# Column sums of two RMS norms: a product with a column of ones, or a transpose and a sum on VectorE

## The chip, the cores and the metric

The kernel runs on one core of a Trainium2 chip. The metric is the device time of one execution in microseconds, as the median of several runs. The engines are TensorE (PE in the profile; PEld is its weight load), VectorE (DVE), ScalarE (ACT), GpSimd (POOL) and SyncE (SP), which here only issues DMAs.

## The reference

One layer of a hybrid model is computed for a prompt of 2048 tokens and a step of 64 tokens, in FP32, with a model width of 1024:

```python
h = rms_norm(x, g_pre)
proj = einsum('btd,dn->btn', h, w_in)              # ten blocks of 1024 columns
...                                                # short convolution (yA), gated recurrence (yB)
merged = sigmoid(gA) * yA + sigmoid(gB) * yB
out = einsum('btd,de->bte', merged, w_o)
x = x + rms_norm(out, g_post)
gate = sigmoid(einsum('btd,de->bte', rms_norm(x, g_ple), w_ple_gate))
x = x + einsum('btp,pd->btd', p, w_ple_proj) * gate

def rms_norm(x, g):
    return x * rsqrt(mean(x * x, axis=-1) + 1e-6) * g
```

The change is in the two norms between w_o and w_ple_gate: the one by g_post and the one by g_ple.

## The kernel before

The 2112 tokens stand side by side and are cut into three blocks of 704, each into two segments (halves) of 352. Activations lie with features on the 128 partitions and tokens along the free axis; a width of 1024 is eight tiles of 128 features. FP32 products are made of three matmuls each on a high and a low part (hi by hi, hi by lo, lo by hi), and large products by a scheme of seven half-size products (functions sgroup, from line 348, and in_turn, from line 469; the three matmuls of one product are lines 362 to 364, 495 to 497 and 528 to 530). Weights come from memory, are split into high and low parts, and the low parts and operand sums of the first block are kept in memory for the later ones.

A norm over features is a sum over partitions here. It is made in steps:

- sum_squares squares the eight feature tiles on ScalarE (lines 634 and 637) and adds them up on VectorE (line 638) into acc, a tile of 128 partitions by tokens.
- col_rstd sums acc over its partitions. For 352 tokens there are three tiles of 128 columns (tiles_of; the third overlaps the second). Each tile is the stationary operand of a product with a column of ones, line 619, so that a column of PSUM gets the sums of 128 tokens, one to a partition. The tokens' sums end as 128 partitions by 3 columns in pc.
- rstd_of scales by 1/1024 and adds epsilon on VectorE (line 590), then takes the power -0.5 on GpSimd (line 592).
- spread (line 603) transposes each column, broadcast to 128x128, so that every partition holds the factor of every token; a copy (line 629, on ScalarE, in the last block on VectorE) brings it to SBUF.
- final_norm multiplies by it: line 1185 with g_post, 1186 adds x, then the second norm, 1199 with g_ple.

rms calls col_rstd once for each segment it is given, and yields between the sums and the spread. In the first and the second block both segments are normed together; in the last block each is normed by itself, so that there are 12 calls of col_rstd.

These steps don't run as a stage of their own. They are handed out by spread_out as hooks, called between the matmuls of the products that follow: in the first two blocks during the gate products of the next block (the first of its stages, lines 362 to 364), in the last block during the end of the W_O products (lines 495 to 497) and during the W_G products of the block before (final_gate, lines 528 to 530). The order on each engine is set by a planner that goes through the program with modelled times and takes by priority what is ready; issue_after pins an instruction behind another on the same engine. With it, placed() queues the products of col_rstd and of spread right behind the last matmul traced before them. DMAs are issued by SP (weights) and by GpSimd (activations, spills, results).

PSUM has five banks for the products (tag pg) and three for everything else (tag pa); pc is one of the latter.

Of the kernel before, what the change touches and what calls it, by code (L numbers as in the profile page):

```python
# [10 lines left out]
F32 = mybir.dt.float32  # L11
# [3 lines left out]
ALU = mybir.AluOpType  # L15
# [3 lines left out]
P = 128  # L19
D = 1024  # L20
# [62 lines left out]
def hybrid_step(  # L83
# [17 lines left out]
    V, A, G, T, SP = nc.vector, nc.scalar, nc.gpsimd, nc.tensor, nc.sync  # L101
# [3 lines left out]
    const = ctx.enter_context(tc.tile_pool(name="const", bufs=1))  # L105
# [13 lines left out]
    def rt(n=BN, dt=F32):  # L119
        t = ring.tile([P, BN + 4], dt, tag="r", name=nm("r"))  # L120
        return t if n is None else t[:, :n]
# [4 lines left out]
    def ps_attn():  # L126
        return psa.tile([P, 512], F32, tag="pa", name=nm("pa"))
# [7 lines left out]

    ident = const.tile([P, P], F32, tag="ident", name="ident")
    make_identity(nc, ident)
    ones = const.tile([P, 1], F32, tag="ones", name="ones")
    V.memset(ones, 1.0)
    mhalf = const.tile([P, 1], F32, tag="mhalf", name="mhalf")  # L140
    V.memset(mhalf, -0.5)
    vec = const.tile([P, 9, KB], F32, tag="vec", name="vec")
# [98 lines left out]
    def placed():  # L241

        return tc.issue_after(last[0]) if last[0] is not None else nullcontext()
# [341 lines left out]
    def tiles_of(n):  # L585

        return [(i, min(i * P, n - P)) for i in range((n + P - 1) // P)]

    def rstd_of(ms_ap, out_ap, scale, start=0):
        scaled = V.tensor_scalar(out_ap, ms_ap, scale, EPS, ALU.mult, ALU.add).ins  # L590
        shape = [out_ap.shape[0], out_ap.shape[1]]
        G.tensor_tensor(out_ap, out_ap, mhalf[start : start + shape[0], :].to_broadcast(shape), ALU.pow)
        return scaled

    def cols_tile(n):
        return small.tile([P, (n + P - 1) // P], F32, tag=f"cols{n}", name=nm("cols"))

    def spread(cols, n):

        pb = ps_attn()  # L600
        with placed():
            for i, o in tiles_of(n):
                T.transpose(pb[:, o : o + P], cols[:, i : i + 1].to_broadcast([P, P]), ident)
        return pb[:, :n]
# [8 lines left out]
    def col_rstd(acc, n):  # L613

        pc = ps_attn()
        cols = cols_tile(n)
        with placed():
            for i, o in tiles_of(n):
                T.matmul(pc[:, i : i + 1], acc[:, o : o + P], ones, start=True, stop=True)
        rstd_of(pc[:, : cols.shape[1]], cols, 1.0 / D)  # L620
        return cols

    def rms(acc, out, segs, copy=A.copy):


        cols = [col_rstd(acc[:, cols_of(sg)], sg["n"]) for sg in segs]
        yield
        for sg, col in zip(segs, cols):
            copy(out[:, cols_of(sg)], spread(col, sg["n"]))
        yield  # L630
# [248 lines left out]
    def cols3(t, nt):  # L879
        return t[:, : nt * P].rearrange("p (g c) -> p g c", c=P)  # L880
# [464 lines left out]
    with behind_all(done):  # L1345
        rs = rt()
        cols = [spread(ss[:, 0, 3 * h : 3 * h + 3], HN) for h in range(2)]
# [22 lines left out]
    for bi, bl in enumerate(blocks):  # L1370
# [6 lines left out]
        cols, a_first = [], []  # L1377
# [18 lines left out]
        mg, xo, h2, acc = [], [], [], rt()  # L1396
# [99 lines left out]
```

## Time and profile before

| | |
|---|---|
| median of three runs | 2632.4 us (2630.19 to 2634.68) |
| profiled execution | 2636.6 us, its span 2634.9 us |
| TensorE busy | 2600.3 us |
| VectorE busy | 1666.3 us |
| ScalarE busy | 1538.5 us |
| GpSimd busy | 386.9 us |

Busy times are of the profiled execution. Times in rows of the timeline are microseconds from the span's start. The first norm begins at 870 us, the last ends at 2539 us. A row of a group gives line, engine, operation, output and inputs by the program's names, the count, and the durations in ns; a row of the timeline gives start, length and what ended the engine's idle time before it, in square brackets.

### The profile page before, as it was taken

The numbers are of one execution on the slowest core, as the hardware profiler recorded it, in microseconds if no ns is written. First come the engines' busy times: TensorE is split into PE (matmuls) and PEld (weight loads), VectorE is DVE, ScalarE is ACT, GpSimd is POOL, SyncE is SP. The second block draws the span as 40 slices with busy tenths as digits, with TensorE's granted clock in tenths as the row PEclk, the third lists the DMA queues.
The fourth block names the chain that finished last, engine by engine and source line by source line (L and its number), as shares of the span: only waits on it lengthen the run. The fifth ranks groups of instructions, "written<-read, shape, count | busy, mean of one in ns | idle before, by whom it ended". The sixth has DMA issues, their size and how long they took to land.

```text
span 2634.9 us, 47400 instructions
## 1 busy us (share of the span) xinstructions
PE 2600.3 (99%) x16550; PEld 2582.7 (98%) x16550; DVE 1666.3 (63%) x3233; ACT 1538.5 (58%) x2948; POOL 386.9 (15%) x713
## 2 busy tenths in 40 slices
PE   7999999999999999999999999999999999999999
PEld 7999999999999999999999999999999999999998
DVE  7687887898777555455545568553455544479656
ACT  5666666554334644677745556466667745565636
POOL 1000000200432210011112211021000101210220
PEclk9999999999999999999999999999999999999999
DMA  8678778898988997767789989599777789989967
GB/s 290 220 262 283 246 269 278 298 316 291 332 299 283 350 328 257 244 224 226 223 288 358 386 306 313 187 363 346 230 228 222 223 258 345 379 308 308 329 234 240
DMA packets 364912, 749.14 MB, mean 284 GB/s; under 512 B 44832, under 2 KB 49472, under 8 KB 364672
## 3 DMA queue, kind: packets, MB, share of 16 engines
q1 hardware_dynamic: 322560, 584.00, 65.2%
q0 software_dynamic: 41824, 162.06, 16.8%
q8 instruction: 130, 2.13, 0.3%
q14 instruction: 110, 0.90, 0.1%
q10 hardware_dynamic: 288, 0.05, 0.0%
HBM read 534.88 MB, written 211.04 MB: 283 GB/s over the span
## 4 chain that ended last, share of the span: by engine, by line
PE 92%; DMA 3%; DVE 2%; issue 1%; ACT 1%; POOL 0%; SPq 0%; ACTq 0%; DVEq 0%; POOLq 0%
PE pg L362 19%; PE pg L364 19%; PE pg L363 19%; PE pg L529 5%; PE pg L530 5%; PE pg L528 5%; PE pg L495 4%; PE pg L496 4%; PE pg L497 4%; PE pa L980 1%; PE pa L944 1%; PE pa L982 1%; PE pa L930 1%; DMA raw<-S 1%; DMA r<-x_fm 1%
## 5 line engine op out<-in xcount | busy, mean ns | idle before, releaser
L362 PE MATMUL pg<-r,hi 128*128 128x352 f32 x3304 | 1094.8, 331 | 4.2 <-DVE r L408 2.6
L363 PE MATMUL pg<-r,hi 128*128 128x352 f32 x3304 | 1068.0, 323 | 0.0
L364 PE MATMUL pg<-r,lo 128*128 128x352 f32 x2356 | 763.2, 324 | 2.2 <-DMA lo<-low 2.2
L218 ACT CAST hi<-raw 128x512 fp32r<-128x512 f32 x720 | 444.3, 619 | 498.8 <-PE pg L363 167.3
L362 PEld LDWEIGHTS pg<-r,hi 128*128 128x128 f32 x3304 | 623.0, 189 | 9.0 <-DVE r L408 4.0
L363 PEld LDWEIGHTS pg<-r,hi 128*128 128x128 f32 x3304 | 623.3, 189 | 0.0
L364 PEld LDWEIGHTS pg<-r,lo 128*128 128x128 f32 x2356 | 443.6, 188 | 2.9 <-DMA lo<-low 2.8
L364 PE MATMUL pg<-r,s 128*128 128x352 f32 x948 | 307.2, 324 | 0.0
L529 PE MATMUL pg<-r,hi 128*128 128x352 f32 x768 | 249.5, 325 | 0.0
L528 PE MATMUL pg<-r,hi 128*128 128x352 f32 x768 | 249.3, 325 | 0.1
L188 ACT CAST hi<-raw 128x512 fp32r<-128x512 f32 x218 | 134.3, 620 | 152.9 <-PE pg L363 46.1
L188 DVE TENSOR_TENSOR r<-r,r 128x352 fp32r<-128x352 f32 (+3 forms) x298 | 183.1, 636 | 63.8 <-ACT r L188 62.9
L496 PE MATMUL pg<-r,hi 128*128 128x352 f32 x672 | 217.3, 325 | 0.0
L495 PE MATMUL pg<-r,hi 128*128 128x352 f32 x672 | 213.6, 325 | 0.1
L530 PE MATMUL pg<-r,lo 128*128 128x352 f32 x656 | 213.0, 325 | 0.0
L188 ACT CAST r<-r 128x352 fp32r<-128x352 f32 (+3 forms) x298 | 161.9, 578 | 61.9 <-DVE r L671 17.4
L188 DVE TENSOR_TENSOR lo<-raw,hi 128x512 fp32r<-128x512 f32 x218 | 149.3, 686 | 68.1 <-ACT hi L188 59.3
L364 PEld LDWEIGHTS pg<-r,s 128*128 128x128 f32 x948 | 178.6, 188 | 0.0
L188 ACT CAST hi<-s 128x512 fp32r<-128x512 f32 x160 | 98.1, 619 | 123.8 <-PE pg L363 112.8
L376 ACT COPY hf<-pg 128x352 f32<-128x352 f32 x354 | 157.0, 446 | 12.2 <-PE pg L364 11.6
L529 PEld LDWEIGHTS pg<-r,hi 128*128 128x128 f32 x768 | 145.2, 189 | 0.4 <-DVE r L188 0.3
L528 PEld LDWEIGHTS pg<-r,hi 128*128 128x128 f32 x768 | 145.1, 189 | 0.4 <-ACT r L188 0.4
(372 smaller groups left out, 4160.5 us busy)
## 6 DMA issues: line engine op xcount, KB each, us to landing
raw<-w_blk SPq DMA_DIRECT2D x570, 256.0 KB, 4.2
lo<-low SPq DMA_DIRECT2D x411, 256.0 KB, 4.4
raw<-S SPq DMA_DIRECT2D x408, 256.0 KB, 4.4
low<-lo SPq DMA_DIRECT2D x322, 256.0 KB, 3.7
s<-low SPq DMA_DIRECT2D x309, 256.0 KB, 4.2
S<-s SPq DMA_DIRECT2D x160, 256.0 KB, 3.1
r<-w_blk POOLq DMA_DIRECT2D x64, 256.0 KB, 7.2
S<-r POOLq DMA_DIRECT2D x64, 256.0 KB, 5.9
```

The lines of the kernel that those rows point to most:

```text
L188: return A.copy(hi, src).ins, V.tensor_tensor(lo, src, hi.bitcast(F32), ALU.subtract).ins
L218: A.copy(hi, raw)
L362: add(hi[:, k, :], xhi, start=start and k == 0, stop=False)
L363: add(hi[:, k, :], xlo, start=False, stop=False)
L364: last[0] = add(lo[:, k, :], xhi, start=False, stop=k == KH - 1).ins
L376: copied = A.copy(got[n], ps[bank])
L495: add(hi[:, k, :], xhi, start=start and k == 0, stop=False)
L496: add(hi[:, k, :], xlo, start=False, stop=False)
L497: last[0] = add(lo[:, k, :], xhi, start=False, stop=k == KH - 1).ins
L528: T.matmul(ps, hi[:, k % 4, :], xhi[:, c], start=k == ks[0], stop=False)
L529: T.matmul(ps, hi[:, k % 4, :], xlo[:, c], start=False, stop=False)
L530: last[0] = T.matmul(ps, lo[:, k % 4, :], xhi[:, c], start=False, stop=k == ks[-1]).ins
```

## The change

Each tile of acc is transposed into PSUM (128 columns for each of the three tiles), so that a token's squares lie along the free axis of one partition; VectorE then adds up each 128, writes 128x3 sums to cols in SBUF, and rstd_of works on cols. The column of ones goes.

```diff
-    ones = const.tile([P, 1], F32, tag="ones", name="ones")
-    V.memset(ones, 1.0)
...
         with placed():
             for i, o in tiles_of(n):
-                T.matmul(pc[:, i : i + 1], acc[:, o : o + P], ones, start=True, stop=True)
-        rstd_of(pc[:, : cols.shape[1]], cols, 1.0 / D)
+                T.transpose(pc[:, i * P : i * P + P], acc[:, o : o + P], ident)
+        nt = cols.shape[1]
+        V.tensor_reduce(cols, cols3(pc, nt), axis=mybir.AxisListType.X, op=ALU.add)
+        rstd_of(cols, cols, 1.0 / D)
         return cols
```

cols3 (line 879 of the kernel before) views the first nt x 128 columns of a tile as 128 x nt x 128.

## The prediction

> **What bounds the kernel now.** I read the profile page first, then the group of each line that the change touches, then the stretches of the timeline around them.
>
> ```profile
> span 2634.9 us, 47400 instructions
> PE 2600.3 (99%) x16550; PEld 2582.7 (98%) x16550; DVE 1666.3 (63%) x3233; ACT 1538.5 (58%) x2948; POOL 386.9 (15%) x713
> PE 92%; DMA 3%; DVE 2%; issue 1%; ACT 1%; POOL 0%; SPq 0%; ACTq 0%; DVEq 0%; POOLq 0%
> ```
>
> TensorE is busy for 99% of the span and makes 92% of the chain that ended last; VectorE has 37% of its time free. So a microsecond taken from TensorE's queue is worth a microsecond wherever TensorE does not then wait for something else, and a microsecond given to VectorE is free unless TensorE waits for its result. The change moves work in exactly that direction.
>
> The lines it touches, by their groups (duration columns are ns min/median/max):
>
> ```profile
> L619 PE MATMUL pa<-ones,r x72: 164/250/353, 870.4 to 2533.1; 128*128 128x1 f32 x72
> L603 PE MATMUL pa<-ident,cols x48: 270/272/421, 793.7 to 2538.8; 128*128 128x128 f32 x48
> L987 DVE TENSOR_REDUCE ms<-r x24: 679/686/689, 123.8 to 2115.7; 128x4 f32<-128x512 f32 x24
> L987 DVE TENSOR_REDUCE ms<-one x24: 276/278/284, 129.9 to 2119.9; 128x1 f32<-128x128 f32 x24
> L590 DVE TENSOR_SCALAR cols<-pa x12: 155/160/163, 871.3 to 2533.5; 128x3 f32<-128x3 f32 x12
> ```
>
> The code calls col_rstd for each of two segments in two norms of three blocks: 12 calls of 3 tiles, 36 products by ones. The trace has 72, so each FP32 product is two passes. The same code's spread (L603) asks for 54 transposes in all and shows 48 under cols, the rest (first block) under another name: a transpose is one pass. It is the very instruction that the change adds, in shape and type.
>
> **What goes and comes on TensorE.** Durations overlap, so I take the pitch: the time by which the next ordinary matmul is late. Timeline of the first norm, both segments together:
>
> ```profile
> 870.15 0.32 PE L363 MATMUL pg<-r,hi 128*128 128x352 f32 x1
> 870.44 1.47 PE L619 MATMUL pa<-ones,r 128*128 128x1 f32 x12
> 872.01 0.32 PE L362 MATMUL pg<-r,hi 128*128 128x352 f32 x1
> ...
> 874.26 0.32 PE L364 MATMUL pg<-r,s 128*128 128x352 f32 x1
> 874.42 0.82 PE L603 MATMUL pa<-ident,cols 128*128 128x128 f32 x6
> 875.24 0.32 PE L363 MATMUL pg<-r,hi 128*128 128x352 f32 x1
> ```
>
> Between the rows at 870.15 and 872.01 one ordinary matmul is folded out, as between 874.26 and 875.24; 874.26 to 874.42 shows the ordinary pitch, 0.16 us. So 12 passes by ones cost 872.01 - 870.15 - 0.32 = 1.54 us, and six transposes 875.24 - 874.26 - 0.32 = 0.66 us. A pair of segments saves 0.88 us. Blocks one and two have two norms each, so four such pairs: 3.5 us. The last block runs its four segments singly:
>
> ```profile
> 2471.76 0.32 PE L497 MATMUL pg<-r,lo 128*128 128x352 f32 x1
> 2472.75 0.32 PE L495 MATMUL pg<-r,hi 128*128 128x352 f32 x1
> ...
> 2474.99 0.32 PE L497 MATMUL pg<-r,lo 128*128 128x352 f32 x1
> 2475.64 0.32 PE L496 MATMUL pg<-r,hi 128*128 128x352 f32 x1
> ```
>
> Six passes: 0.99 - 0.32 = 0.67 us; three transposes: 0.65 - 0.32 = 0.33 us; 0.34 us saved each. If nothing absorbed any of it, TensorE would gain 3.5 + 4 x 0.34 = 4.9 us, 0.19%.
>
> [...]
>
> **What comes on VectorE.** Twelve reductions of 128x384 to 128x3, from PSUM. From the two rows of L987, (686 - 278) / 384 = 1.06 ns an element, so 278 + 256 x 1.06 = 550 ns; 12 of them are 6.6 us. Those rows read SBUF; PSUM is not shown for a reduction, so the bounds are 0.28 us (the 128-element row) and 0.69 us (the 512-element row). I take 0.55. The scale-and-epsilon step (0.16 us) stays and reads SBUF instead of PSUM, at no cost that I can see. The memset of the ones goes, once, in the start-up: nothing.
>
> In the first norm this is covered:
>
> ```profile
> 871.95 0.16 DVE L590 TENSOR_SCALAR cols<-pa 128x3 f32<-128x3 f32 x1 [0.51 <-PE pa L619]
> 871.52 1.72 POOL L592 TENSOR_TENSOR cols<-cols,mhalf 128x3 f32<-128x3 f32 x2 [17.84 <-DVE cols L590]
> ```
>
> VectorE now idles for TensorE ahead of these. With the change the first three transposes land about 0.49 us after 870.44 (the length of three in the last block's timeline), and two reductions and two scalings follow: 870.44 + 0.49 + 2 x 0.55 + 2 x 0.16 = 872.35 instead of 872.11. GpSimd's two powers are one block of 1.72 us, now ending at 873.24; the second, of 0.86, would end about 873.3. TensorE reaches the spread at 874.26 - 0.88 = 873.38, and uses the second column only three transposes later. The cover is thin, about 0.1 us; gone, each further 0.1 us of reduction would cost TensorE 0.1 us at this place and at its twin in the second block. Behind the reduction on VectorE queue the sums that empty the matmul banks; they come at 872.68 today, after another idle stretch.
>
> **What is late next.** Pairs two and four (the g_ple norms) start when acc is ready, and that is not TensorE's doing:
>
> ```profile
> 1754.80 9.89 DMA raw<-S
> 1767.50 0.90 DVE r L638
> 1768.54 1.47 PE pa L619 x12
> 900.00:910.00 10.00, 10.00 (x64) 1.00 1.04 405
> 1760.00:1770.00 10.00, 9.32 (x61) 1.00 1.04 398
> ```
>
> The first three rows are from the chain that ended last: a weight load of 9.89 us holds ScalarE, whose squares wait in its queue, then the sum of L638, then the norm. In the windows (last columns: granted clock, DMA share, GB/s) the 16 DMA engines are full, in both blocks. TensorE arrives with nothing to spare, so what pairs one and three give may be waited away at pairs two and four: between 0 and 1.76 us is left. Neither end is nearer, and I take half, 0.88. Pairs two and four keep their 1.76: no wait of such a size follows until this one, which goes along with TensorE's own progress through the weights:
>
> ```profile
> PE pg L364 <- DMA lo<-low: 2.2, 2, 2.0
> 1050.00:1060.00 10.00, 7.96 (x44) 0.89 0.95 315
> 1060.00:1070.00 10.00, 10.00 (x69) 0.94 0.76 265
> ```
>
> The last block ends in a wait of its own:
>
> ```profile
> 2498.06 0.35 PEld L603 LDWEIGHTS pa<-ident,cols 128*128 128x128 f32 x3
> 2496.91 1.10 POOL L592 TENSOR_TENSOR cols<-cols,mhalf 128x3 f32<-128x3 f32 x1 [11.97 <-DVE cols L590]
> 2532.16 1.27 PE L619 MATMUL pa<-ones,r 128*128 128x1 f32 x6 [4.75 <-DVE r L638]
> ```
>
> At 2498 the power ends at 2498.01 and the spread starts at 2498.06: no slack, so a reduction of 0.55 us there is a stall of 0.55. At 2532 TensorE waits 4.75 us for VectorE, so whatever TensorE saved between 2470 and 2532 is absorbed, and VectorE's additions of about 0.6 us count (one reduction late, the next partly offset by the shorter transposes ahead of it). Against that the last single saves half of its 1.27 us, 0.64, at a low clock. The last block nets 0, between -1.4 (four singles saved) and +1.7 us (three reductions in the chain).
>
> **The sum.** 0.88 + 1.76 + 0 = 2.6 us less. The profiled execution took 2636.6 us (span 2634.9 and 1.7 around it), 4.2 us over the median of 2632.4; the saving taken off it gives 2634.0, and off the median **2629.8 us**. With the bounds above the forecast's own range is 2627.5 (3.5 of the pairs and 1.4 of the last block, 4.9 in all) to 2632.3 (the 1.76 kept, 1.7 lost in the last block). A measurement of this kernel can tell about 0.2%, 5.3 us, from no change, so this counts as the same.
>
> **Rivals.**
>
> *Everything absorbed.* The code does remove the passes, but if the full DMA engines set the pace around all four pairs, nothing arrives: 2632.4 us. For it: DMA share 1.04. Against: TensorE idles under 1 us in each of those windows.
>
> *Faster.* The saving arrives whole and takes a clock drop with it.
>
> ```profile
> 870.00:880.00 10.00, 10.00 (x68) 1.00 0.97 335
> 1770.00:1780.00 10.00, 10.00 (x56) 0.83 0.99 358
> ```
>
> Right behind the fourth pair the granted clock is 0.83 over 10 us: 1.7 us lost. The first pair, with nearly no wait ahead, has no such drop (1.00 from 870 on); the fourth had a wait plus 1.47 us of one-column matmuls. Transposes halve that. 4.9 + 1.7 = 6.6 us: 2625.8. If the planner also moves the last norm earlier, part of the 4.75 us goes too: down to about 2621.
>
> *Slower: a new order.* Order within an engine is planned from modelled times, apart from what is pinned. The rows at 1050 price a badly timed load: 2.0 us of wait and then 0.11 + 0.06 of ten microseconds at a lower clock, 1.7 us; 3.7 in all. New durations on three engines from 870 on can shift which weight load is asked for first. From the third such stall on it decides: 2632.4 - 2.6 + 11.1 = 2640.9. Against it, a long stage as planned now:
>
> ```profile
> 1060.00:1700.00 640.00, 639.79 (x4137) 1.00 0.81 275
> ```
>
> TensorE is idle there for 0.2 us of 640.
>
> *Slower: the clock.* If transposes do not hold the clock, each norm is followed by a drop like that at 1770. Two of the eight groups have one now; six more at 1.7 us, less 2.6, give +7.6: 2640.0. Against: after the six transposes at 874.42 the clock stays at 1.00 in the window quoted. [...]
>
> **How the numbers follow.** Forecast 0.33, all absorbed 0.08, faster 0.29, new order 0.24, clock 0.06. Faster by over 0.2%: 0.29 and a rim of the forecast, 0.30. Slower: 0.24 + 0.06 = 0.30. Within: 0.40. The range takes the forecast, the nearer part of the faster case and the third stall: 2623 to 2641; beyond it lie the planner's largest gift and a fourth stall, under 0.2.
>
> **What the profile after would show.** L617's transposes x36 at 272 ns and no pass by ones; a reduction x12 near 0.55 us; the pairs at about 0.66 us by pitch. Waits at the second and fourth pair: larger if absorbed. The drop at 1770: gone in the faster case. TensorE's waits for DMA: more in the case of a new order. The forecast is wrong if TensorE's idle time changes by more than its work does, or if six transposes take over 1 us.

## The result and the profile after

| | before | after |
|---|---|---|
| median of 20 runs each | 2632.35 us | 2625.98 us |
| lowest to highest | 2629.08 to 2635.73 | 2622.47 to 2632.90 |
| profiled execution, its span | 2636.6, 2634.9 us | 2629.7, 2628.0 us |
| mean granted clock of the runs | 0.9969 (33 runs, beside the first four experiments) | 0.9976 |

The ratio is 0.9978, 95% interval 0.9971 to 0.9985: 5.8 us less by the ratio, 6.4 by the medians, where 2.6 was forecast and 6.6 belonged to the rival "faster". A second series of the changed kernel (below) gives 0.9983, 0.9974 to 0.9992, or 4.5 us. So it is faster by about 0.2%, at the edge of what counted as the same.

The page of the changed kernel: span, busy time of each engine, shares of the chain that ended last.

```profile
span 2628.0 us, 47342 instructions
PE 2590.4 (99%) x16514; PEld 2570.7 (98%) x16514; DVE 1671.0 (64%) x3244; ACT 1540.0 (59%) x2948; POOL 389.0 (15%) x713
PE 90%; DVE 3%; DMA 3%; issue 2%; ACT 1%; POOL 0%; SPq 0%; ACTq 0%; DVEq 0%; POOLq 0%
```

TensorE has 36 instructions fewer and is busy 9.9 us less, VectorE 4.7 us more. Up to 6.8 of the 9.9 us are the clock, an estimate: leaving out the last 10 us, the profile before has 23.9 us at half clock, the one after 10.2, and half of the difference is 6.8. The new instructions, by line (ns min/median/max; the last row is from the costliest groups: busy us, mean ns):

```profile
L617 PE MATMUL pa<-ident,r x36: 270/272/301, 869.8 to 2527.4; 128*128 128x128 f32 x36
L619 DVE TENSOR_REDUCE cols<-pa x12: 548/554/558, 870.3 to 2527.9; 128x3 f32<-128x384 f32 x12
L590 POOL TENSOR_TENSOR cols<-cols,mhalf 128x3 f32<-128x3 f32 x12 | 11.8, 990 | 64.7 <-DVE cols L588 64.7
```

There is one transpose of 272 ns for each tile, and a reduction of 0.554 us where 0.55 was estimated. What TensorE waited for at the sums and at the spreads (us in total, times, longest):

```profile
PE pa L617 <- DVE r L638: 2.9, 1, 2.9
PE pa L601 <- POOL cols L590: 1.9, 3, 0.8
```

The wait ahead of the last norm has fallen from 4.75 to 2.9 us, and a wait for GpSimd's powers has appeared, three times. Two of the three are the g_post pairs. The first of them:

```profile
869.75 0.85 PE L617 MATMUL pa<-ident,r 128*128 128x128 f32 x6
870.31 1.02 DVE L619 TENSOR_REDUCE cols<-pa 128x3 f32<-128x384 f32 x2 [0.70 <-PE pa L617]
871.25 0.16 DVE L588 TENSOR_SCALAR cols<-cols 128x3 f32<-128x3 f32 x1
871.31 0.51 DVE L399 TENSOR_TENSOR hf<-hf,pg 128x352 f32<-128x352 f32 x1
871.49 1.99 POOL L590 TENSOR_TENSOR cols<-cols,mhalf 128x3 f32<-128x3 f32 x2 [18.49 <-DVE cols L588]
871.74 0.16 DVE L588 TENSOR_SCALAR cols<-cols 128x3 f32<-128x3 f32 x1
872.43 0.54 PE L601 MATMUL pa<-ident,cols 128*128 128x128 f32 x3
873.53 0.54 PE L601 MATMUL pa<-ident,cols 128*128 128x128 f32 x3 [0.56 <-POOL cols L590]
```

Both reductions stand ahead of the first scale, so the first power starts 1.74 us after the first transpose (before: 1.08 after the first pass by ones); the second segment's spread waits 0.56 us. At the g_ple pairs the spread comes later and nothing waits:

```profile
917.79 0.82 PE L617 MATMUL pa<-ident,r 128*128 128x128 f32 x6
918.31 1.02 DVE L619 TENSOR_REDUCE cols<-pa 128x3 f32<-128x384 f32 x2 [1.32 <-PE pa L617]
919.50 1.71 POOL L590 TENSOR_TENSOR cols<-cols,mhalf 128x3 f32<-128x3 f32 x2 [1.69 <-DVE cols L588]
922.31 0.82 PE L601 MATMUL pa<-ident,cols 128*128 128x128 f32 x6
```

### The profile page after: what moved, and what is told of

Same layout as the page of the kernel before. It is cut to its first block, busy times and chain, and to the rows that moved or that the text cites. A ratio compares the mean times of both kernels' runs of the same rounds, so it can differ in the third digit from the quotient of the medians.

```text
span 2628.0 us, 47342 instructions
## 1 busy us (share of the span) xinstructions
PE 2590.4 (99%) x16514; PEld 2570.7 (98%) x16514; DVE 1671.0 (64%) x3244; ACT 1540.0 (59%) x2948; POOL 389.0 (15%) x713
## 4 chain that ended last, share of the span: by engine, by line
PE 90%; DVE 3%; DMA 3%; issue 2%; ACT 1%; POOL 0%; SPq 0%; ACTq 0%; DVEq 0%; POOLq 0%
PE pg L360 20%; PE pg L362 20%; PE pg L361 20%; PE pg L528 4%; PE pg L527 4%; PE pg L526 4%; PE pg L494 3%; PE pg L493 3%; PE pg L495 3%; PE pa L944 1%; PE pa L980 1%; PE pa L982 1%; PE pa L930 1%; DMA r<-x_fm 1%; DMA lo<-low 1%
```

## How the experiments are read

Executions of one kernel lie some 10 us apart at the most, so the times alone can't tell 1 us. Each experiment is therefore read in its trace too, as the time between the same two ordinary matmuls: counted in order of start without the sums' own, numbers 5300 to 5500 enclose the first g_post pair, 10700 to 10900 the second, 5300 to 5760 both pairs of the first block, 10700 to 11200 both of the second, 15500 to 16000 the four singles of the last block. "Wait" is TensorE's ahead of the last norm, "half" the stretch at half clock that follows it, in the trace's record of the granted clock. Microseconds throughout; the ratio is to the kernel before on the same chip.

| kernel | ratio (95%) | post 1 | post 2 | pairs 1, 2 | pairs 3, 4 | last | wait | half |
|---|---|---|---|---|---|---|---|---|
| before | 1 | 34.66 | 34.59 | 77.80 | 86.65 | 91.06 | 4.8 | 6.8 |
| changed | 0.9978 (0.9971-0.9985) | 34.82 | 34.76 | 77.78 | 83.75 | 87.32 | 2.9 | 3.4 |
| changed again (e12) | 0.9983 (0.9974-0.9992) | 34.81 | 34.75 | 78.20 | 83.42 | 86.86 | 2.5 | 3.4 |
| e1 blocks 1, 2 only | 0.9990 (0.9981-0.9998) | 34.82 | 34.75 | 77.52 | 84.34 | 90.53 | 4.3 | 6.8 |
| e2 last block only | 0.9990 (0.9981-0.9998) | 34.66 | 34.60 | 79.20 | 85.13 | 87.84 | 3.5 | 3.4 |
| e3 g_ple pairs only | 0.9994 (0.9985-1.0003) | 34.68 | 34.58 | 77.52 | 84.27 | 89.59 | 4.1 | 6.8 |
| e4 g_post pairs only | 1.0002 (0.9993-1.0011) | 34.82 | 34.75 | 77.82 | 84.96 | 89.69 | 4.2 | 6.8 |
| e5 last norm only | 0.9994 (0.9985-1.0003) | 34.66 | 34.59 | 78.66 | 84.59 | 89.01 | 4.8 | 3.4 |
| e6 first three singles | 0.9992 (0.9983-1.0000) | 34.66 | 34.60 | 77.90 | 85.54 | 90.16 | 4.3 | 6.8 |
| e7 sum behind scale | 0.9982 (0.9973-0.9991) | 34.87 | 34.81 | 77.71 | 83.72 | 87.81 | 3.4 | 3.4 |
| e8 one power | 0.9975 (0.9965-0.9986) | 34.64 | 34.59 | 77.85 | 83.52 | 85.43 | 2.2 | 0 |
| e9 scale first | 0.9986 (0.9978-0.9995) | 34.34 | 34.28 | 77.09 | 83.35 | 87.94 | 3.7 | 3.4 |
| e10 spread later | 0.9995 (0.9986-1.0004) | 34.20 | 34.10 | 77.87 | 85.82 | 87.47 | 3.2 | 3.4 |
| e11 later, one power | 0.9995 (0.9985-1.0004) | 34.01 | 33.93 | 79.32 | 84.61 | 87.51 | 3.3 | 3.4 |

## Which of the twelve norms bring it

The first six kernels choose between the two ways by the number of the call of col_rstd (0 and 1 are the first g_post pair, 2 and 3 the first g_ple pair, 4 to 7 the second block's, 8 to 11 the last block's singles):

```diff
+        turn_n = len(calls)
+        calls.append(n)
...
+                if turn_n in (0, 1, 2, 3, 4, 5, 6, 7):
+                    T.transpose(pc[:, i * P : i * P + P], acc[:, o : o + P], ident)
+                else:
+                    T.matmul(pc[:, i : i + 1], acc[:, o : o + P], ones, start=True, stop=True)
```

with (8, 9, 10, 11) for e2, (2, 3, 6, 7) for e3, (0, 1, 4, 5) for e4, (11,) for e5 and (8, 9, 10) for e6.

**e1, blocks one and two.** Expected:

> Transposes and reductions in the four pairs of blocks one and two, products by ones in the four singles of the last block. Theory (the savings at the g_post pairs are given back at their spreads, those at the g_ple pairs stay, and the low clock behind the fourth pair goes): 1.7 from the g_ple pairs and 1.7 from the clock, 3.4 us less than before; the wait ahead of the last norm stays near 4.8 us. Rival one (every pair keeps its 0.88): 3.5 + 1.7 = 5.2 us less. Rival two (the gain is all the last block's): no difference.

**e2, the last block.** Expected:

> Products by ones in blocks one and two, transposes and reductions in the four singles of the last block. Theory: the wait ahead of the last norm falls from 4.8 to about 2.9 us and the half clock behind it from 6.8 to 3.4 us: about 3.0 to 3.5 us less than before; the low clock behind the fourth pair (0.83 over 1770 to 1780) stays. Rival one (only the four singles' 0.34): 1.4 us less. Rival two (the gain is all the last block's): 6.4 us less.

**e3, the g_ple pairs.** Expected:

> Transposes and reductions only in the two g_ple pairs of blocks one and two. Theory and rival one alike: 1.7 us by pitch and 1.7 by the clock behind the fourth pair, which is 1.00 over 1770 to 1780: 3.4 us less than before. No wait of TensorE at those pairs' spreads. Rival two: no difference. If the low clock there is chance and not the work of the products by ones, 1.7 us less.

**e4, the g_post pairs.** Expected:

> Transposes and reductions only in the two g_post pairs of blocks one and two. Theory: each pair saves 0.88 us and TensorE waits that long at its spread for GpSimd's powers (two waits of 0.5 us or more by line 601's successor): 0 +- 0.5 us against before, and the low clock behind the fourth pair stays. Rival one: 1.8 us less.

Measured, by the ratios: 2.6, 2.6, 1.6 less and 0.5 more, each +-2.3. These times alone hardly separate the theories: that the gain is the last block's alone is only just excluded by them (e1's interval ends at 0.9998), and more plainly by the column of pairs 3 and 4. That every pair keeps its 0.88 is refuted by the g_post columns: wherever the g_post pairs were changed and nothing else was done about them, each is 0.15 to 0.17 us longer than before (34.82 against 34.66), not shorter. The wait that pays for it, in e4:

```profile
PE pa L603 <- POOL cols L592: 1.1, 2, 0.6
```

The g_ple pairs keep theirs: pairs 3 and 4 together take 84.27 in e3 and 84.96 in e4, on one profile each; the means are given further down.

The clock part of my rival "faster" falls here, and with it that part of this theory. The low clock of 0.83 right behind the fourth pair was to go with the products by ones. In e2 and e5, which still have them there, it is not low (granted clock is the third number from the end):

```profile
1770.00:1780.00 10.00, 10.00 (x66) 9.97 (x65) 4.97 (x8) 5.82 (x11) 1.14 (x2) 1.00 1.02 382
```

```profile
1770.00:1780.00 10.00, 10.00 (x66) 9.97 (x65) 5.11 (x8) 5.48 (x12) 1.66 (x3) 1.00 1.03 375
```

Of five profiles with ones at that place (before, e2, e4, e5, e6) one shows the drop, of nine with transposes none. The changed kernel's own row:

```profile
1770.00:1780.00 10.00, 10.00 (x66) 9.97 (x65) 4.59 (x8) 5.63 (x11) 2.32 (x4) 1.00 1.05 395
```

It is no rule of the old kernel; whether ones make it likelier can't be told from five (what it goes with in the kernel before stands in the next section). The same holds for a drop near 1058 us, in five of the fourteen profiles, of both kinds. Without its 1.7 us the old pairs 3 and 4 take 84.95.

## The last block: a wait and a clock

**e5, only the very last norm.** Expected:

> Transpose and reduction only in the very last norm of a segment (the one at 2532 us); products by ones in the other eleven. Theory one (the half clock behind that norm is set by its own one-column products): half clock of 3.4 instead of 6.8 us, the wait ahead still about 4.2 to 4.8 us; 1.7 by the clock and 0.3 to 0.6 by the products, 2.0 to 2.3 us less than before, mean clock of the runs 0.9977. Theory two (it goes with the length of the wait ahead): half clock still 6.8 us, at most 0.6 us less, mean clock 0.9969 as before.

**e6, only the three before it.** Expected:

> Transposes and reductions in the first three singles of the last block (2472 to 2502 us); products by ones in blocks one and two and in the very last norm. Theory one: the wait ahead of the last norm may fall to 3.5 us or less by VectorE's changed order, but the half clock behind it stays at 6.8 us: 0.3 to 1.3 us less than before. Theory two: wait of 2.9 to 3.5 us and half clock of 3.4 us, 2.5 to 3 us less, mean clock 0.9977.

Here are the last norms of e5 and of e6, and 10 us of each from about that point:

```profile
2527.59 0.87 PE L624 MATMUL pa<-ident,r 128*128 128x128 f32 x3 [4.80 <-DVE r L650]
```

```profile
2527.00:2537.00 10.00, 9.41 (x52) 9.42 (x53) 6.47 (x13) 2.25 (x6) 3.58 (x6) 0.83 0.65 219
```

```profile
2528.02 1.41 PE L626 MATMUL pa<-ones,r 128*128 128x1 f32 x6 [4.29 <-DVE r L650]
```

```profile
2527.00:2537.00 10.00, 8.98 (x42) 8.98 (x43) 4.81 (x10) 1.84 (x5) 4.20 (x6) 0.67 0.58 201
```

The longer wait has the shorter low clock. Before and after the change it is nearly the same pair of numbers, 0.66 and 0.83:

```profile
2532.00:2542.00 10.00, 9.84 (x45) 9.80 (x45) 4.53 (x10) 1.16 (x3) 4.20 (x6) 0.66 0.62 225
```

```profile
2527.00:2537.00 10.00, 9.81 (x54) 9.81 (x54) 6.09 (x13) 1.96 (x5) 3.59 (x6) 0.83 0.69 239
```

In the table "half" is 6.8 us in all five kernels whose last norm has products by ones, 3.4 in eight and 0 in one of the nine with transposes. In times e5's 1.6 us (-0.8 to 3.9) and e6's 2.1 (0.0 to 4.5) cannot tell theory one from two, nor can the mean clocks of their runs, 0.9974 and 0.9973; the traces do.

The clock record of the traces bears on this. In each of the fourteen, every drop begins a whole number of 3.413 us after the drop before it (in the kernel before 6, 294, 209, 223 and 29 of them, in the changed one 300, 431 and 29). So each trace can be divided into intervals of 3.413 us, with bounds at which all its drops begin. Here are such intervals, the first low one at the last norm and the one after it, in the kernel before and in e5 (TensorE's busy time and matmuls, then the clock):

```profile
2532.31:2535.72 3.41, 3.41 (x14) 0.50 0.42 162
2535.72:2539.13 3.41, 3.41 (x14) 0.50 0.48 155
```

```profile
2527.25:2530.66 3.41, 3.07 (x12) 0.50 0.54 205
2530.66:2534.07 3.41, 3.41 (x24) 1.00 0.53 178
```

In the kernel before, the low interval has no idle time and 1.12 us of one-column passes, and the next is low too. In e5 it has 0.34 us of idle time, 0.87 us of transposes and not more ordinary matmuls (2.2 us of them instead of 2.3), and yet the next is at full clock. e1 is like the former, e2, e9 and e11 like the latter: with the bounds at nearly the same place the half clock lasts 6.8 us with one-column passes and 3.4 with transposes, as theory one has it. One low interval more costs half of 3.4 us, an estimated 1.7. The runs agree: their mean clock is 0.99697 over the 140 runs of kernels with ones in the last norm and 0.99764 over the 105 with transposes, which is 1.8 us of 2630, though these kernels differ in other places too.

But where the bounds fall differs too, and no run varied it alone. In e3, e4 and e6 the first low interval also holds 1.2 to 1.7 us of the wait. In the changed kernel, e7, e10 and e12 it begins when the transposes are over, or nearly (0.14 us of them are left in e10). In e8 a bound falls into the middle of the wait of 2.2 us, and no half clock follows (1.00 from 2522 to 2532 us). At the fourth pair of the kernel before, the interval ahead of the low clock at 1771 us holds 0.47 us of wait and all 1.47 us of passes; in e2, e4 and e6, where no drop follows, the same passes come with 0.03 to 0.15 us of wait, in e5, also without a drop, a bound parts them from the wait. What brings the clock down in the next interval is shown by no run.

The wait is the other part. With the three norms before it changed, the planner puts VectorE's work from about 2500 to 2520 us in another order. The waits of VectorE for the loads of x in that stretch, in the kernels before, after and e6:

```profile
DVE r L1186 <- DMA r<-x_fm: 5.2, 2, 2.8
```

```profile
DVE r L1186 <- DMA r<-x_fm: 2.5, 3, 1.6
```

```profile
DVE r L1198 <- DMA r<-x_fm: 2.5, 3, 1.9
```

They are 4.5 to 5.2 us in the five kernels with ones in those three norms and 1.7 to 2.8 in the nine with transposes. TensorE's wait is 2.2 to 4.3 us (mean 3.21) instead of 4.1 to 4.8 (mean 4.45). What joins the two is one load of x, issued by GpSimd (a pair of loads, of which it is the first). Before, and after the change:

```profile
2519.78 1.09 POOL L1176 DMA_DIRECT2D r<-x_fm  x2
2525.15 0.53 DVE L1186 TENSOR_TENSOR r<-r,r 128x352 f32<-128x352 f32 x1 [2.38 <-DMA r<-x_fm]
```

```profile
2513.66 1.09 POOL L1176 DMA_DIRECT2D r<-x_fm  x2
2520.19 0.53 DVE L1186 TENSOR_TENSOR r<-r,r 128x352 f32<-128x352 f32 x1 [0.72 <-DMA r<-x_fm]
```

In all fourteen profiles the last norm's sums on TensorE begin 7.0 us after this addition. Counted from matmul 15500, GpSimd issues the load at 59.7 to 60.2 us in the five kernels with ones in the three norms and at 56.7 to 57.9 in the nine with transposes. So the earlier issue comes from those three norms. What it is worth is not fixed: the load takes 5.4 us to land in the kernel before, 6.5 in the changed one and 6.7 in e6, which has the new order and still waits 4.3 us, as e1, e3 and e4 do without it (4.1 to 4.3).

Together, the four singles take 87.3 us on the mean of changed, e2 and e12, and 90.2 on that of before, e1, e3 and e4: 2.9 less. Of this, 1.42 us are the shorter wait and 1.45 come behind it, by the clock and the shorter passes together. The three singles ahead of the wait give nothing: in all fourteen TensorE reaches it 67.3 to 67.4 us after matmul 15500, since the second single's spread, 1.0 us longer with its stall, takes what three times 0.33 us of shorter sums give.

## Why the g_post pairs gave nothing

In the changed kernel VectorE takes a bank-emptying sum (line 399) between the two scales. **e7** moves it behind:

```diff
-        V.tensor_tensor(t, x, y, ALU.add)
+        with behind_all(scales):
+            V.tensor_tensor(t, x, y, ALU.add)
...
-        rstd_of(cols, cols, 1.0 / D)
+        scales[:] = [rstd_of(cols, cols, 1.0 / D)]
```

> The changed kernel, with VectorE's bank-emptying sum (line 399 of the changed kernel) pinned behind the second segment's scale step, so that the scale follows the reductions at once. Theory (the g_post pairs' saving was given back because that sum stood ahead of the second scale, and GpSimd's second power and with it the spread came late): the second wait of TensorE at each g_post spread falls from 0.54 to at most 0.1 us, 0.5 to 1.7 us less than the changed kernel, 6 to 8 us less than before. Rival (the spread is late by the reduction's own 0.55 us, whatever stands behind it): the waits stay at 0.4 us or more and the time is the changed kernel's.

```profile
867.48 0.29 DVE L590 TENSOR_SCALAR cols<-cols 128x3 f32<-128x3 f32 x2
867.73 2.04 POOL L592 TENSOR_TENSOR cols<-cols,mhalf 128x3 f32<-128x3 f32 x2 [18.48 <-DVE cols L590]
869.82 0.54 PE L603 MATMUL pa<-ident,cols 128*128 128x128 f32 x3 [0.62 <-POOL cols L592]
```

My theory fell: the second scale now follows at once, and the wait is 0.62 instead of 0.56. GpSimd does the two powers one after the other in 2.04 us; the second scale had never been late for it.

**e8** gives both segments of a pair one scale and one power, with e7's pin:

```diff
...
+        for sg, col in zip(segs, cols):
+            col_sums(acc[:, cols_of(sg)], sg["n"], col)
+        scales[:] = [rstd_of(both, both, 1.0 / D)]
```

> As the kernel with the sum pinned, and one scale and one power for both segments of a pair (128x6 instead of twice 128x3), in blocks one and two. Theory: reductions end 1.1 us after the first transposes land, one scale of 0.16 and one power of about 0.9 us follow, so the spread's second half no longer waits and its first half waits up to 0.5 us; 0.5 to 1.7 us less than the changed kernel. Rival (a power's time goes with its columns, so one of six lasts as long as two of three): the first half of the spread waits 0.9 us more and the gain is lost, the time is the changed kernel's or up to 1 us above it.

```profile
867.37 1.36 POOL L592 TENSOR_TENSOR cols<-cols,mhalf 128x6 f32<-128x6 f32 x1 [18.61 <-DVE cols L590]
868.79 0.87 PE L603 MATMUL pa<-ident,cols 128*128 128x128 f32 x6 [0.52 <-POOL cols L592]
```

The power of six columns takes 1.36 us, between the two cases (0.9 and 1.8), and the whole spread now waits 0.52. Each g_post pair is as long as before the change (34.64), so 0.17 us is won at each, less than expected. Its ratio of 0.9975 is not told apart from the changed kernel's 0.9978; in its profile the last block is 1.9 us shorter than the changed kernel's, with a wait of 2.2 us and no half clock behind it. The edit does not touch that block's singles: of all fourteen, its addition of x comes earliest (62.6 us after matmul 15500), and a bound of the intervals of 3.413 us happens to part the wait.

Two causes were left: GpSimd starts late because both reductions go first (A), and TensorE comes early, because the planner now puts the spread 12 ordinary matmuls behind the sums where it had 16 (B). Why it does is not shown; a modelled time of the new steps that is too short would do it.

**e9** pins the second reduction behind the first scale:

```diff
-        V.tensor_reduce(cols, cols3(pc, nt), axis=mybir.AxisListType.X, op=ALU.add)
-        rstd_of(cols, cols, 1.0 / D)
+        with behind_all(scales):
+            V.tensor_reduce(cols, cols3(pc, nt), axis=mybir.AxisListType.X, op=ALU.add)
+        scales[:] = [rstd_of(cols, cols, 1.0 / D)]
```

> The changed kernel with the second reduction of a pair pinned behind the first segment's scale (reduction, scale, reduction, scale instead of reduction, reduction, scale, scale). Theory A (the planner's order on VectorE makes GpSimd's first power, and so the second, late): the first power starts about 0.45 us earlier, the wait of TensorE at the g_post spreads falls from 0.56 to 0.0 to 0.2 us. Theory B (TensorE comes too early: the planner put the spread 12 matmuls behind the sums where it had 16, 4 x 0.16 = 0.64 us): the wait falls too, but part of it stays, and each g_post stretch gains less than 0.45 us. Time against the changed kernel: 0 to 1 us less, not to be told by the times alone.

```profile
868.77 0.85 PE L618 MATMUL pa<-ident,r 128*128 128x128 f32 x6
869.33 0.56 DVE L621 TENSOR_REDUCE cols<-pa 128x3 f32<-128x384 f32 x1 [0.70 <-PE pa L618]
870.00 0.55 DVE L621 TENSOR_REDUCE cols<-pa 128x3 f32<-128x384 f32 x1
870.17 1.84 POOL L591 TENSOR_TENSOR cols<-cols,mhalf 128x3 f32<-128x3 f32 x2 [18.16 <-DVE cols L589]
872.07 0.54 PE L602 MATMUL pa<-ident,cols 128*128 128x128 f32 x3 [0.20 <-POOL cols L591]
```

The first power starts 1.40 us after the first transpose instead of 1.74, the wait falls from 0.56 to 0.20, and each g_post pair is 0.48 us shorter than in the changed kernel (34.34 against 34.82).

**e10** moves the hook of the g_post spreads until 16 matmuls stand in between:

```diff
-            spread_out((norm, (0, 1, 0, 1) + (0, 1, 0) * KB + (0, 1, 0, 1) + (0, 1) * KB))
+            spread_out((norm, (0, 1, 0, 0, 0, 0, 0, 1, 1) + (0, 1, 0) * 7 + (1, 0, 1) + (0, 1) * KB))
```

> The changed kernel with the hook of the g_post spreads moved, so that 16 ordinary matmuls stand between sums and spread as before the change, not 12. Theory B: the wait at these spreads falls from 0.56 to 0.15 us or less, and the stretch around each g_post pair is 0.5 to 0.9 us shorter than before the change (it is 0.15 longer in the changed kernel). Theory A: the wait stays at 0.4 us or more. Second question, whether a microsecond won there arrives: if full DMA engines pace the first block's pairs, the stretch over both of them (products 5300 to 5760) stays at 77.5 to 77.9 us; if not, it falls to about 76.9.

```profile
866.07 0.85 PE L617 MATMUL pa<-ident,r 128*128 128x128 f32 x6
869.33 1.05 PE L601 MATMUL pa<-ident,cols 128*128 128x128 f32 x6
```

No wait is shown there any more, though the six transposes take 1.05 us instead of 0.82, and each g_post pair is 0.46 to 0.49 us shorter than before the change. So both causes are real: either mends most of the wait and leaves about 0.2 us. But the hooks also move the g_ple sums by 12 matmuls, and there TensorE now waits for the sums of squares (three waits at the sums, the longest of them the last norm's):

```profile
PE pa L617 <- DVE r L638: 5.5, 3, 3.2
```

Pairs 3 and 4 end up at 85.82, no better than before.

**e11** has both the one power and the later spread.

> Both: one scale and one power for a pair, the sum of line 399 pinned behind the scale, and the g_post spreads 16 matmuls behind the sums. No wait at these spreads (0.5 us with the power alone); each g_post stretch 0.6 to 0.9 us shorter than before the change. 1 to 2 us less than the changed kernel if it arrives, 0 to 0.5 if the DMA engines pace the pairs.

Its g_post pairs are the shortest of all, 0.65 us under before. The first block's pairs together still take 79.32 us, 1.5 more than before. TensorE's waits for weights in the whole run, of the low parts and the operand sums kept in memory:

```profile
PE pg L363 <- DMA lo<-low: 3.0, 2, 2.0
PE pg L363 <- DMA s<-low: 2.6, 2, 1.4
```

Of these, 0.96 and 1.41 us stand between the first pair and the second (at 891.5 and 895.2 us); the rest is elsewhere. So what was won at the first pair was lost before the second here, and e10 has less of the same (pairs 1 and 2 at 77.87 with 0.46 won at the first). That this is the absorption by full DMA engines that the forecast allowed for is not shown: e2, with nothing changed in that block, waits 1.01 us there too and takes 79.20, and the stretch lies between 77.1 and 79.3 in all fourteen, whichever way the sums are made.

**e12** is the changed kernel again.

> The changed kernel once more, beside the three above: 5 to 6.5 us less than before. The granted clock from 1770 to 1780 is 1.00 (the low clock there in the profile before was chance: kernels with products by ones at that place did not show it), the half clock behind the last norm lasts 3.4 us, the mean clock of the runs is 0.9976 to 0.9980 against 0.9969.

4.5 us less by the ratio, just under what was expected; no low clock at 1770; mean clock 0.9978 as expected, against 0.9972 of the kernel before, which had 0.9969 in the series beside e1 to e8. No version was shown to beat the changed kernel.

## Why the prediction came out as it did

- **The time and the range.** The time lies within the stated range, 3.8 us under the forecast, but that says little for the sum, since the range of 18 us took in several of the rivals. Of the sum's terms the four pairs gave 1.6 us where 2.6 was put down, and the last block 2.9 where 0 was: two misses of opposite sign, and that the total is off by less than the last block alone is luck. By the signs of being wrong that it named the forecast stands: TensorE's idle time grew by 3.0 us where its busy time fell by 9.9, and six transposes take 0.82 to 0.85 us.
- **What goes on TensorE.** Passes and transposes are as counted (72 and 36). The 0.88 us is right at the first g_ple pair (0.67 us by pitch instead of 1.55) and too large at the g_post pairs. There my 1.54 us for the ones contains the short gap ahead of the first pass, which the transposes keep (0.82 by pitch); the 0.66 us for the transposes came from a spread without one. Where next to no wait is left (e11), a g_post pair is 0.65 us shorter than before.
- **What comes on VectorE.** 0.55 us was right (0.554).
- **The cover at the g_post pairs.** I called it thin, 0.1 us, and left nothing for it in the sum. Here the step failed: I set reduction, scale, reduction, scale, and the spread where it had been. The planner put both reductions first and the spread four matmuls earlier. The wait is 0.56 us, and these two pairs net +0.15 each, where 0.44 each was kept in the sum.
- **What is late next.** The g_ple pairs keep their saving, as said, in the second block: pairs 3 and 4 take 83.9 us on the mean of changed, e1, e3 and e12 against 85.0 of the kernels with ones at the g_ple pair (before without its drop, e2, e4, e5, e6), 1.1 less. In the first block 77.8 against 78.3, within their scatter. Of the forecast's 2.6 for the four pairs some 1.6 is there.
- **The last block.** Mis-sized: 0 was the forecast, with -1.4 as its best; it is -2.9. The stall at the second single came as said (0.8 us, the longest of the three at the spreads, where 0.55 was put down), and with it the first three singles gave nothing. Two terms were missed. The first is the half clock behind the last norm: I credited the transposes with 0.64 us for being shorter at a low clock, not with a low clock that ends 3.4 us sooner; both together gave 1.45 us. The second is the planner's new order, with which the last load of x that is waited for is issued some 3 us earlier and the wait is 1.42 us shorter on the mean; "the planner's largest gift" stood in the rival.
- **The rivals.** "Faster" gave the time (2625.8) by a wrong road: 4.9 us of passes that did not all arrive, and a low clock at 1770 that one profile in five has. "New order" as a loss did not happen: from 2.2 us for two waits on low parts before to 2.2 for two after. The clock rival is refuted: clocks are 1.00 behind the transposes of the four pairs and the first three singles, and the last norm's low clock is half as long with them (3.4 us against 6.8). That is for this length, 0.82 to 0.85 us of transposes between dense matmuls at a pair. One transpose is 272 ns long, and that is not the time it takes up: six take 0.82 to 0.85 us.

The sum by the traces: 0.5 + 1.1 + 2.9 = 4.5 us, against 5.8 (3.9 to 7.6) and 4.5 (2.1 to 6.8) measured.

## What to carry to other kernels

Where a planner sets the order, price an edit with the order that it will choose for the new steps: here it moved the consumer up by four matmuls, and the whole saving of two pairs went into a wait. A short stretch of thin products right after an idle stretch may go with a loss longer than itself: with 1.27 us of one-column passes behind a wait of 4.75 us the kernel before had 6.8 us of half clock, e5 with transposes there 3.4 behind 4.80. A wait is traced to its end before it is priced: the last norm's hung on one load, 7.0 us ahead. And a low clock that one profile shows is a sample: look for it in a second one of the same code before it enters a sum.

## What the runs showed of the hardware

- The granted clock dropped to half for stretches of 3.41 us or twice that (leaving out the last 10 us), and every drop began a whole number of 3.413 us after the one before it (fourteen traces). Behind a wait of 4.1 to 4.8 us the half clock lasted 6.8 us with six one-column passes in between (before, e1, e3, e4, e6), 3.4 us with three transposes behind a wait of 4.8 (e5); a wait of 2.2 us, parted by a bound into 1.1 and 1.1, had none (e8, one profile), one of 2.45 in a single interval had 3.4 (e12). An interval of 3.413 us with 1.12 us of one-column passes in it was followed by another at half clock (the kernel before), one with 0.87 us of transposes and 0.34 idle by full clock (e5); what sets the clock of an interval was not shown.
- A power of 128x6 on GpSimd takes 1.36 us, two of 128x3 take 1.71 to 2.04 together. The second of two lasted 1.12 us in the changed kernel and 0.85 in e9, both with VectorE at work beside it; why is open.
